# Column means of an 8192 x 8192 matrix: a quarter of the last adds on GpSimd, and the rows loaded in other blocks

## The chip, the core and the metric

The kernel runs on one core of a Trainium2 chip. Its time is device time in microseconds (us), from runs on the chip; lower is better. The engines named here are VectorE (DVE in the profile), GpSimd (POOL), TensorE (PE, with its weight loads as PEld), ScalarE (ACT) and SyncE (SP), which only issues transfers here. SBUF is the on-chip memory, of 128 partitions; PSUM takes TensorE's results. Sixteen DMA engines move data between HBM and SBUF.

## The reference

```python
def reference(x):                 # x: (8192, 8192) float32, standard normal
    return np.mean(x, axis=0)     # 8192 column means
```

All of the 268 MB of `x` has to be read once; the output has 32 KB.

## The kernel before, in words

A *slab* is 128 rows, one in each partition, and so 4 MB in SBUF. There are 64 slabs (`n_slabs`). The first 62 are loaded as 31 *pairs* (`n_pairs`), each of 8 MB: 128 partitions times two rows side by side, 16384 columns, into one of three buffers `pair0` to `pair2` (L48) in turn. Then come slab 62 (`slab`) and slab 63 (`last`), both into the buffer after pair 30's.

**Which rows a pair holds** is free, since all rows are summed. `source` (L78) says it. Rows 0 to 8063 are nine blocks of 7 x 128 rows (`RUN`, L20): partition p has seven rows that lie one after the other in HBM, 224 KB. Pairs 0 to 26 are the first six rows of each partition, two at a time, so a partition's part is one run of 64 KB. The seventh rows of the nine blocks (`single`, L75) make pairs 27 to 30, two blocks for a pair, and slab 62; their runs are 32 KB or less. Slab 63 is the last 128 rows.

**Transfers.** `cuts` (L85) says in how many transfers a pair comes. Pair 0 comes in two, issued by ScalarE (L102 and L139). Pairs 1 to 24 come whole. Pairs 25 to 30 (`BY_ROW`, L19) come by row, 4 MB each, and the last of them in four pieces of half a row. Slab 62 comes in two halves (L161), slab 63 in eight pieces (`PIECES`, L17): 2048, 2048, 2048, 1408, 192, 288, 96 and 64 columns. Apart from pair 0's, all are issued on SP's queue by `load` (L137, L139), in this order. The first transfer of a pair waits until its buffer is free: until the pair three before has been added to the next one (`freed` in the loop, `freed_by` on the semaphore `dve` behind it). What stands behind a waiting transfer on SP waits too.

**VectorE adds.** The running sum moves along: for pair k, an add puts the sum so far (first 8192 columns of the previous buffer) onto the first row of pair k, and a second add puts the second row of pair k onto that. In SBUF, pair k's first 8192 columns are then the sum. Pairs 1 to 24 (`LOOPED`, L21) are in a loop on VectorE (L179 to L189); the rest is the list `adds` (L116 to L134), issued at L192 to L198, each add waiting for the one before it by `dve`. All adds have line L173. At last slab 62 is added to `total` in four parts of 2048 columns, each noted in `done`.

**TensorE ends it.** Matrix products with a column of ones add up over the partitions into PSUM. The columns are four wide parts (2048, 2048, 2048, 1408) and four narrow ones. `open_wide(n)` (L234) waits for `done[n]` and puts `total`'s part into PSUM; `close` (L226) waits for the part's piece of slab 63 and adds it. The order is: some products on zeros (L241, which wait for the second add before `done[0]`), open 0, open 1, close 0, open 2, close 1, open 3 and the narrow ones, close 2, close 3, close narrow (L244 to L256). ScalarE and VectorE multiply by 1/8192 (L266, L269) and four transfers store the result.

GpSimd does nothing in this kernel but four memsets of one column at the start.

Of the kernel before, what the change touches and what calls it, by code (L numbers as in the profile page):

```python
# [7 lines left out]
F32 = mybir.dt.float32  # L8
ADD = mybir.AluOpType.add
MULT = mybir.AluOpType.mult  # L10
P = 128
# [4 lines left out]
NARROW = (192, 288, 96, 64)  # L16
PIECES = WIDE + NARROW  # L17
FIRST = 2048
BY_ROW = 6  # L19
RUN = 7  # L20
LOOPED = 24  # L21


@with_exitstack
def kernel(
# [5 lines left out]
    nc = tc.nc  # L31
    R, C = x.shape
    n_slabs = R // P
    n_pairs = n_slabs // 2 - 1
    N0 = sum(WIDE)
    H = C // 2
    assert n_slabs % 2 == 0 and N0 + sum(NARROW) == sum(PIECES) == C
    assert LOOPED % 3 == 0 and LOOPED < n_pairs - 1
    inv_r = 1.0 / float(R)

    const_pool = ctx.enter_context(tc.tile_pool(name="const", bufs=1))
    psum_pool = ctx.enter_context(
        tc.tile_pool(name="acc", bufs=1, space=bass.MemoryType.PSUM)
    )
    res_pool = ctx.enter_context(tc.tile_pool(name="res", bufs=1))

    ones = const_pool.tile([P, 32], F32, name="ones")
    bufs = [nc.alloc_sbuf_tensor(f"pair{b}", [P, 2 * C], F32, align_bytes=512).ap() for b in range(3)]  # L48
    banks = [psum_pool.tile([P, 512], F32, name=f"bank{b}", tag=f"bank{b}") for b in range(8)]
    rw = nc.alloc_sbuf_tensor("rw", [P, 3 * 512], F32).ap()  # L50
    r3 = nc.alloc_sbuf_tensor("r3", [P, WIDE[3] // GROUPS], F32).ap()
    row = nc.alloc_sbuf_tensor("row", [P, C - N0], F32).ap()[0:1, :]
    idle = res_pool.tile([P, 512], F32, name="idle")

    wide, lo = [], 0
    for n, w in enumerate(WIDE):
# [9 lines left out]

    n_blocks = (R - P) // (P * RUN)
    n_whole = n_blocks * (RUN // 2)  # L70
    assert R == (n_blocks * RUN + 1) * P and 2 * n_whole + n_blocks == 2 * n_pairs + 1
    assert LOOPED < n_whole
    blocks = x[0 : R - P, :].rearrange("(b p j) c -> b p (j c)", p=P, j=RUN)

    def single(n, lo, hi):  # L75
        return blocks[n, :, (RUN - 1) * C + lo : (RUN - 1) * C + hi]

    def source(k, lo, hi):  # L78
        if k < n_whole:
            b, t = divmod(k, RUN // 2)  # L80
            return blocks[b, :, 2 * t * C + lo : 2 * t * C + hi]
        j = lo // C
        return single(2 * (k - n_whole) + j, lo - j * C, hi - j * C)

    def cuts(k):  # L85
        if k == 0:
            return [(0, FIRST), (FIRST, 2 * C)]
        if k < n_pairs - BY_ROW:
            return [(0, 2 * C)]
        step = H if k == n_pairs - 1 else C  # L90
        return [(lo, lo + step) for lo in range(0, 2 * C, step)]

    def untracked(ap, size):

# [2 lines left out]
    sem = nc.alloc_semaphore  # L97
    landed = [sem(f"landed{b}") for b in range(3)]
    first = sem("first")


    early = nc.scalar.dma_start(out=untracked(bufs[0][:, 0:FIRST], 2 * C * P), in_=source(0, 0, FIRST))  # L102
    early.then_inc(first, 16)
    tc.no_tile_sem_insts.add(early.ins.name)
# [4 lines left out]
    with tc.tile_critical(sync_engine=mybir.EngineType.Pool) as section:  # L109
        tc.declare_no_dep(section, early.ins, reason="awaited by first")  # L110
        freed, half = sem("freed"), sem("half")
        dve, act, pe = sem("dve"), sem("act"), sem("pe")
        came = {}


        adds, freed_by = [], {}  # L116
        for k in range(LOOPED + 1, n_pairs):
            pair, before = bufs[k % 3], bufs[(k - 1) % 3]
            pieces = cuts(k)
            for n, (lo, hi) in enumerate(pieces):  # L120
                if lo < C:
                    adds.append(((k, n), pair[:, lo:hi], before[:, lo:hi]))
                else:
                    adds.append(((k, n), pair[:, lo - C : hi - C], pair[:, lo:hi]))
                if hi == C:
                    freed_by[k - 1] = len(adds)
        total = bufs[(n_pairs - 1) % 3]
        slab = bufs[n_pairs % 3][:, 0:C]
        last = bufs[n_pairs % 3][:, C : 2 * C]
        parts = [(lo, lo + 2048) for lo in range(0, C, 2048)]  # L130
        done = []
        for lo, hi in parts:
            adds.append((("slab", lo // H), total[:, lo:hi], slab[:, lo:hi]))
            done.append(len(adds))  # L134


        def load(key, dst, src, after=None):  # L137

            ld = (nc.scalar if key[0] == 0 else nc.sync).dma_start(out=dst, in_=src)  # L139
            if after is not None:  # L140
                ld.wait_op(after[0], after[1], "sem-ge")
            if key not in came:
                came[key] = sem(f"came_{'_'.join(map(str, key))}")
            ld.then_inc(came[key], 16)

        for k in range(n_pairs):
            for n, (lo, hi) in enumerate(cuts(k)):
                after = None
                if k >= 3 and n == 0:
                    f = k - 3  # L150
                    after = (freed, f + 1) if f < LOOPED else (dve, freed_by[f])
                if k == 1:
                    after = (first, 16)
                key = (k, n)
                if k <= LOOPED:
                    came[key] = first if (k, n) == (0, 0) else landed[k % 3]
                if key == (0, 0):
                    continue
                load(key, bufs[k % 3][:, lo:hi], source(k, lo, hi), after)
        r = (n_slabs - 2) * P  # L160
        for n in range(2):  # L161
            after = (dve, freed_by[n_pairs - 3]) if n == 0 else None
            load(("slab", n), slab[:, n * H : n * H + H], single(n_blocks - 1, n * H, n * H + H), after)
        at, lo = {}, 0
        for n, w in enumerate(PIECES):
            load(("last", n), last[:, lo : lo + w], x[r + P : R, lo : lo + w])
# [5 lines left out]
        def vadd(a, b):  # L172
            return nc.vector.tensor_tensor(out=a, in0=a, in1=b, op=ADD)  # L173
# [5 lines left out]
        with nc.vector.register("left") as left:  # L179
            nc.vector.reg_mov(left, LOOPED // 3)  # L180
            with nc.vector.While(lambda: nc.vector.snap(left) > 0):
# [9 lines left out]
        awaited = None  # L191
        for n, (key, a, b) in enumerate(adds):  # L192
            if key != awaited:
                nc.vector.wait_ge(came[key], 16)
                awaited = key
            add = vadd(a, b).then_inc(dve, 1)
# [2 lines left out]
        n_dve = len(adds)  # L199


        n_pe = 0

        def mm(dst, src, **flags):
# [2 lines left out]
        def fold_wide(n, src, **flags):  # L207
            lo, w, bank = wide[n]
            q = w // GROUPS
            for g in range(GROUPS):  # L210
                a = lo + g * q
                m = mm(bank[32 * g : 32 * g + 32, 0:q], src[:, a : a + q], **flags)
            return m
# [12 lines left out]
        def close(fold, n, lo):  # L226
            nonlocal n_pe
            landed_at(lo)
            fold(n, last, start=False, stop=n != narrow[2]).then_inc(pe, 1)
            n_pe += 1  # L230
            return n_pe

        ready = {}
        def open_wide(n):  # L234
            nc.tensor.wait_ge(dve, done[n])
            fold_wide(n, total, start=True, stop=False)


        nc.tensor.wait_ge(dve, done[0] - 2)
        for _ in range(4):  # L240
            nc.tensor.matmul(  # L241
                out=banks[7][:, 0:512], lhsT=idle[:, 0:P], rhs=idle, start=True, stop=True, skip_group_check=True
            )
        open_wide(0)  # L244
        open_wide(1)
        ready["wide", 0] = close(fold_wide, 0, wide[0][0])
        open_wide(2)
        ready["wide", 1] = close(fold_wide, 1, wide[1][0])
        nc.tensor.wait_ge(dve, done[3])
        fold_wide(3, total, start=True, stop=False)  # L250
        for part in (*narrow[:2], ending):
            fold_narrow(part, total, start=True, stop=False)
# [24 lines left out]
        for n, (engine, part) in enumerate(  # L277
            ((nc.scalar, narrow[0]), (nc.vector, narrow[1]), (nc.scalar, ending))
        ):
            lo, w, g, bank, _ = part  # L280
            awaited = ready["narrow", 3 if part is ending else n]
# [68 lines left out]
```

## Time and profile before

| what | us |
|---|---|
| median of 3 runs (lowest, highest) | 627.12 (627.09, 627.58) |
| the profiled execution: time | 627.51 |
| its span, first to last instruction | 625.7 |
| VectorE busy, 67 adds (L173) among it | 541.3, 539.7 |
| VectorE waiting for transfers | 73.7, in 22 waits |
| TensorE busy | 13.6 |
| 4 MB transfers (10), issue to landing, median | 27.6 |

The page has a row for each group of instructions: line, engine, operation, output and input, their shapes, how often; behind the bar the busy time of the group and the mean time of one in ns; behind the second bar the idle time of the engine ahead of them and what ended it. The map of the span has 40 slices, with the busy share in tenths. A timeline's rows begin with start and duration in us, and merge instructions that follow on one another ("x9"). A row of the table of stretches has the stretch, its length, busy time and count for PE, PEld, DVE, ACT and POOL, the granted TensorE clock, the share of the DMA engines and GB/s. The chain of waits goes back from the last instruction to what released each one.

### The profile page before, as it was taken

Reading aid. Unit: us, or ns where it says so; the run is one execution under the profiler, and the core shown is the slowest. Engines: PE = TensorE matmul, PEld = TensorE weight load, DVE = VectorE, ACT = ScalarE, POOL = GpSimd, SP = SyncE. Lnnn points to the kernel's source line nnn. Section 1 sums busy time; section 2 is a strip of 40 time slices with the busy share of each in tenths; the row PEclk is TensorE's granted clock in tenths of the full one; section 3 lists DMA queues with packets and bytes.
Section 4 is the critical chain, followed back from the end, with each engine's and each line's share of the span. In section 5 each row is a group of like instructions: output and inputs, shape, how many; then the busy total and the mean of one; then the engine's idle time right before and its main releaser. Section 6 shows DMA issues by size and latency. Waiting matters only on the chain.

```text
span 625.7 us, 475 instructions
## 1 busy us (share of the span) xinstructions
PE 13.6 (2%) x86; PEld 4.6 (1%) x86; DVE 541.3 (87%) x71; ACT 3.7 (1%) x6; POOL 0.2 (0%) x4
## 2 busy tenths in 40 slices
PE   0000000000000000000000000000000000000025
PEld 0000000000000000000000000000000000000011
DVE  0049999989888899888898888988889899999996
ACT  0000000000000000000000000000000000000001
POOL 0000000000000000000000000000000000000000
PEclk9999999999999999999999999999999999999999
DMA  9999999999999999999999999999999999999997
GB/s 377 436 461 402 469 402 469 402 469 402 469 402 469 402 432 440 402 469 402 469 402 469 402 469 402 469 402 469 402 465 406 432 425 419 434 436 436 434 422 320
DMA packets 7231, 268.48 MB, mean 429 GB/s; under 512 B 1069, under 2 KB 1329, under 8 KB 1470
## 3 DMA queue, kind: packets, MB, share of 16 engines
q1 hardware_dynamic: 6940, 260.08, 96.2%
q10 hardware_dynamic: 290, 8.39, 3.2%
q14 instruction: 1, 0.01, 0.0%
HBM read 268.44 MB, written 0.03 MB: 429 GB/s over the span
## 4 chain that ended last, share of the span: by engine, by line
DMA 59%; DVE 39%; issue 0%; SPq 0%; DVEq 0%; PE 0%; ACTq 0%
DMA pair<-in_x_dram 59%; DVE pair L173 39%; SPq L139 0%; PE bank L205 0%; DVE r L269 0%; DVEq L109 0%; ACTq L102 0%; DVEq L186 0%; DVEq L184 0%; DVEq L173 0%; ACTq L345 0%
## 5 line engine op out<-in xcount | busy, mean ns | idle before, releaser
L173 DVE TENSOR_TENSOR pair<-pair 128x8192 f32<-128x8192 f32 (+2 forms) x67 | 539.7, 8056 | 78.0 <-DMA pair<-in_x_dram 73.7
L241 PE MATMUL bank<-idle 128*128 128x512 f32 x8 | 5.3, 817 | 605.6 <-DVE pair L173 605.6
L205 PE MATMUL bank<-pair,ones 128*32 128x512 f32 (+5 forms) x78 | 8.4, 523 | 3.8 <-DVE pair L173 3.6
L241 PEld LDWEIGHTS bank<-idle 128*128 128x128 f32 x8 | 2.1, 276 | 607.9 <-DVE pair L173 605.6
L266 ACT ACTIVATE rw<-bank 128x512 f32<-128x512 f32 x3 | 1.8, 597 | 617.3 <-PE bank L205 617.3
L269 DVE TENSOR_SCALAR r<-bank 128x352 f32<-128x352 f32 x1 | 0.5, 525 | 3.2 <-PE bank L205 3.2
L205 PEld LDWEIGHTS bank<-pair,ones 128*32 128x32 f32 x78 | 2.5, 108 | 10.2 <-DVE pair L173 7.1
L266 ACT ACT_TABLE_LOAD x1 | 1.3, 1283 | 1.8 <-issue 1.8
L175 DVE MEMSET ones<- 128x32 f32 x1 | 0.1, 85 | 1.0 <-PEq L334 1.0
L266 ACT ACTIVATE row<-bank 1x192 f32<-1x192 f32 (+1 forms) x2 | 0.6, 308 | 0.7 <-PE bank L205 0.7
L176 DVE MEMSET idle<- 128x512 f32 x1 | 0.5, 485 | 0.1
L269 DVE TENSOR_SCALAR row<-bank 1x288 f32<-1x288 f32 x1 | 0.4, 448 | 0.0
L334 POOL MEMSET const-bfloat16-1.0<- 128x1 bf16 x1 | 0.1, 101 | 0.0
L334 POOL MEMSET const-uint8-127<- 128x1 uint8 x1 | 0.1, 101 | 0.0
L334 POOL MEMSET const-float32-0.0<- 128x1 f32 x1 | 0.1, 98 | 0.2 <-issue 0.2
L334 POOL MEMSET const-float32-1.0<- 128x1 f32 x1 | 0.1, 98 | 0.0
## 6 DMA issues: line engine op xcount, KB each, us to landing
pair<-in_x_dram SPq DMA_DIRECT2D x10, 4096.0 KB, 27.6
pair<-in_x_dram SPq DMA_DIRECT2D x6, 2048.0 KB, 28.4
pair<-in_x_dram ACTq DMA_DIRECT2D x1, 7168.0 KB, 37.9
pair<-in_x_dram SPq DMA_DIRECT2D x3, 1024.0 KB, 33.4
pair<-in_x_dram ACTq DMA_DIRECT2D x1, 1024.0 KB, 4.7
pair<-in_x_dram SPq DMA_DIRECT2D x1, 704.0 KB, 36.6
pair<-in_x_dram SPq DMA_DIRECT2D x24, 29.8
pair<-in_x_dram SPq DMA_DIRECT2D x1, 144.0 KB, 30.2
```

The lines of the kernel that those rows point to most:

```text
L173: return nc.vector.tensor_tensor(out=a, in0=a, in1=b, op=ADD)
L175: nc.vector.memset(ones, 1.0)
L176: nc.vector.memset(idle, 0.0)
L205: return nc.tensor.matmul(out=dst, lhsT=ones, rhs=src, skip_group_check=True, **flags)
L241: nc.tensor.matmul(out=banks[7][:, 0:512], lhsT=idle[:, 0:P], rhs=idle, start=True, stop=True, skip_group_check=True)
L266: op = engine.mul(out=dst, in_=src, mul=inv_r).then_inc(act, 1)
L269: op = engine.tensor_scalar(out=dst, in0=src, scalar1=inv_r, scalar2=None, op0=MULT).then_inc(dve, 1)
L334: nc = _bacc.Bacc("TRN2", target_bir_lowering=False, num_devices=1)
```

## The change

- `RUN` is 6: ten blocks of 6 x 128 rows (7680 rows) make pairs 0 to 29, all in runs of 64 KB. The step from one partition's rows to the next one's is 192 KB. Pair 30 is the next 256 rows, two in each partition (`two`), slab 62 the next 128 rows as they lie, slab 63 the last 128.
- Pairs 1 to 29 come whole. Pair 30 comes by row, in two transfers; slab 62 comes in one.
- The loop on VectorE goes to pair 27 (`LOOPED`). Pair 28 is added as before, in adds of 8192 columns.
- For pairs 29 and 30, VectorE adds columns 0 to 4095 and 6144 to 8191, and GpSimd columns 4096 to 6143 (`SHARE`), with a semaphore `gp` of its own. For slab 62, VectorE has three parts of 2048 and GpSimd that of `SHARE`, which is `open_wide(2)`'s.
- GpSimd waits first for VectorE's adds of pair 28 (`whole`), then for each landing, and each add for its own one before.
- SP's load of slab 62 waits for GpSimd's first add as well as for VectorE's.
- `idle` (the zeros of L241) lies in another pool; nothing else is done to it.

```diff
-BY_ROW = 6
-RUN = 7
-LOOPED = 24
+RUN = 6
+LOOPED = 27
+SHARE = (4096, 6144)
...
+    per_block = RUN // 2
+    n_blocks = (n_pairs - 1) // per_block
+    R0 = n_blocks * RUN * P
+    blocks = x[0:R0, :].rearrange("(b p j) c -> b p (j c)", p=P, j=RUN)
+    two = x[R0 : R0 + 2 * P, :].rearrange("(p j) c -> p (j c)", j=2)
 
     def source(k, lo, hi):
-        if k < n_whole:
-            b, t = divmod(k, RUN // 2)
-            return blocks[b, :, 2 * t * C + lo : 2 * t * C + hi]
-        j = lo // C
-        return single(2 * (k - n_whole) + j, lo - j * C, hi - j * C)
+        if k == n_pairs - 1:
+            return two[:, lo:hi]
+        b, t = divmod(k, per_block)
+        return blocks[b, :, 2 * t * C + lo : 2 * t * C + hi]
 
     def cuts(k):
         if k == 0:
             return [(0, FIRST), (FIRST, 2 * C)]
-        if k < n_pairs - BY_ROW:
-            return [(0, 2 * C)]
-        step = H if k == n_pairs - 1 else C
-        return [(lo, lo + step) for lo in range(0, 2 * C, step)]
+        return [(0, C), (C, 2 * C)] if k == n_pairs - 1 else [(0, 2 * C)]
...
+        adds, shared, freed_by = [], [], {}
+        outer = ((0, SHARE[0]), (SHARE[1], C))
         for k in range(LOOPED + 1, n_pairs):
-            pair, before = bufs[k % 3], bufs[(k - 1) % 3]
-            pieces = cuts(k)
-            for n, (lo, hi) in enumerate(pieces):
-                if lo < C:
-                    adds.append(((k, n), pair[:, lo:hi], before[:, lo:hi]))
+            now, before = bufs[k % 3], bufs[(k - 1) % 3]
+            final = len(cuts(k)) - 1
+            for piece, src, lo in ((0, before, 0), (final, now, C)):
+                if k < n_pairs - 2:
+                    adds.append(((k, piece), now[:, 0:C], src[:, lo : lo + C]))
                 else:
-                    adds.append(((k, n), pair[:, lo - C : hi - C], pair[:, lo:hi]))
-                if hi == C:
+                    for a, b in outer:
+                        adds.append(((k, piece), now[:, a:b], src[:, lo + a : lo + b]))
+                    a, b = SHARE
+                    shared.append(((k, piece), now[:, a:b], src[:, lo + a : lo + b]))
+                if not lo:
                     freed_by[k - 1] = len(adds)
+            if k == n_pairs - 3:
+                whole = len(adds)
...
-        for lo, hi in parts:
-            adds.append((("slab", lo // H), total[:, lo:hi], slab[:, lo:hi]))
-            done.append(len(adds))
+        for lo in range(0, C, 2048):
+            cols = slice(lo, lo + 2048)
+            if (lo, lo + 2048) == SHARE:
+                shared.append((("slab", 0), total[:, cols], slab[:, cols]))
+                done.append((gp, len(shared)))
+            else:
+                adds.append((("slab", 0), total[:, cols], slab[:, cols]))
+                done.append((dve, len(adds)))
...
-        for n in range(2):
-            after = (dve, freed_by[n_pairs - 3]) if n == 0 else None
-            load(("slab", n), slab[:, n * H : n * H + H], single(n_blocks - 1, n * H, n * H + H), after)
+        nc.sync.wait_ge(gp, 1)
+        load(("slab", 0), slab, x[r : r + P, :], (dve, freed_by[n_pairs - 3]))
...
+        nc.gpsimd.wait_ge(dve, whole)
+        awaited = None
+        for n, (key, a, b) in enumerate(shared):
+            if key != awaited:
+                nc.gpsimd.wait_ge(came[key], 16)
+                awaited = key
+            add = nc.gpsimd.tensor_tensor(out=a, in0=a, in1=b, op=ADD).then_inc(gp, 1)
+            if n:
+                add.wait_op(gp, n, "sem-ge")
...
         def open_wide(n):
-            nc.tensor.wait_ge(dve, done[n])
+            nc.tensor.wait_ge(*done[n])
```

More of the change, by code (lines that the diff above doesn't have):

```diff
@@ L35 @@
     N0 = sum(WIDE)
-    H = C // 2
     assert n_slabs % 2 == 0 and N0 + sum(NARROW) == sum(PIECES) == C
-    assert LOOPED % 3 == 0 and LOOPED < n_pairs - 1
+    assert LOOPED % 3 == 0 and LOOPED < n_pairs - 2
     inv_r = 1.0 / float(R)
@@ L44 @@
     )
-    res_pool = ctx.enter_context(tc.tile_pool(name="res", bufs=1))
     ones = const_pool.tile([P, 32], F32, name="ones")
+    idle = const_pool.tile([P, 512], F32, name="idle")
     bufs = [nc.alloc_sbuf_tensor(f"pair{b}", [P, 2 * C], F32, align_bytes=512).ap() for b in range(3)]
@@ L52 @@
     row = nc.alloc_sbuf_tensor("row", [P, C - N0], F32).ap()[0:1, :]
-    idle = res_pool.tile([P, 512], F32, name="idle")
     wide, lo = [], 0
@@ L65 @@
     ending = (narrow[2][0], sum(NARROW[2:]), narrow[2][2], narrow[2][3], 0)
[L69 to L76, printed above, removed]
-    def source(k, lo, hi):
-        if k < n_whole:
-            b, t = divmod(k, RUN // 2)
-            return blocks[b, :, 2 * t * C + lo : 2 * t * C + hi]
-        j = lo // C
-        return single(2 * (k - n_whole) + j, lo - j * C, hi - j * C)
+    per_block = RUN // 2
+    n_blocks = (n_pairs - 1) // per_block
+    R0 = n_blocks * RUN * P
+    assert n_blocks * per_block == n_pairs - 1 and R == R0 + 4 * P
+    blocks = x[0:R0, :].rearrange("(b p j) c -> b p (j c)", p=P, j=RUN)
+    two = x[R0 : R0 + 2 * P, :].rearrange("(p j) c -> p (j c)", j=2)
+    def source(k, lo, hi):
+        if k == n_pairs - 1:
+            return two[:, lo:hi]
+        b, t = divmod(k, per_block)
+        return blocks[b, :, 2 * t * C + lo : 2 * t * C + hi]
     def cuts(k):
@@ L111 @@
         freed, half = sem("freed"), sem("half")
-        dve, act, pe = sem("dve"), sem("act"), sem("pe")
+        dve, act, pe, gp = sem("dve"), sem("act"), sem("pe"), sem("gp")
         came = {}
-        adds, freed_by = [], {}
+        adds, shared, freed_by = [], [], {}
+        outer = ((0, SHARE[0]), (SHARE[1], C))
         for k in range(LOOPED + 1, n_pairs):
-            pair, before = bufs[k % 3], bufs[(k - 1) % 3]
-            pieces = cuts(k)
-            for n, (lo, hi) in enumerate(pieces):
-                if lo < C:
-                    adds.append(((k, n), pair[:, lo:hi], before[:, lo:hi]))
-                else:
-                    adds.append(((k, n), pair[:, lo - C : hi - C], pair[:, lo:hi]))
-                if hi == C:
+            now, before = bufs[k % 3], bufs[(k - 1) % 3]
[3 more added lines that the diff above has]
+                    adds.append(((k, piece), now[:, 0:C], src[:, lo : lo + C]))
+                else:
+                    for a, b in outer:
[3 more added lines that the diff above has]
+                if not lo:
                     freed_by[k - 1] = len(adds)
+            if k == n_pairs - 3:
+                whole = len(adds)
         total = bufs[(n_pairs - 1) % 3]
@@ L129 @@
         last = bufs[n_pairs % 3][:, C : 2 * C]
-        parts = [(lo, lo + 2048) for lo in range(0, C, 2048)]
         done = []
-        for lo, hi in parts:
-            adds.append((("slab", lo // H), total[:, lo:hi], slab[:, lo:hi]))
-            done.append(len(adds))
+        for lo in range(0, C, 2048):
[6 more added lines that the diff above has]
+                done.append((dve, len(adds)))
         def load(key, dst, src, after=None):
@@ L234, in open_wide @@
         def open_wide(n):
-            nc.tensor.wait_ge(dve, done[n])
+            nc.tensor.wait_ge(*done[n])
             fold_wide(n, total, start=True, stop=False)
-        nc.tensor.wait_ge(dve, done[0] - 2)
+        nc.tensor.wait_ge(dve, done[0][1] - 2)
         for _ in range(4):
@@ L248 @@
         ready["wide", 1] = close(fold_wide, 1, wide[1][0])
-        nc.tensor.wait_ge(dve, done[3])
+        nc.tensor.wait_ge(*done[3])
         fold_wide(3, total, start=True, stop=False)
```

## The prediction, on record before the result

> **What bounds the kernel now.** I read the page's busy shares, the chain of waits, the groups by form, the timeline of the last 40 us, and table-of-stretches answers for the transfer rate.
>
> ```profile
> PE 13.6 (2%) x86; PEld 4.6 (1%) x86; DVE 541.3 (87%) x71; ACT 3.7 (1%) x6; POOL 0.2 (0%) x4
> DMA  9999999999999999999999999999999999999997
> ...
> DMA 59%; DVE 39%; issue 0%; SPq 0%; DVEq 0%; PE 0%; ACTq 0%
> ```
> The DMA engines are full in every slice but the last: 268.4 MB move from 1.30 us (first transfer of the chain) to 621.63 us, 433 GB/s. The chain names DVE for 39% only because a free buffer and a landing alternate in it; no slice shows the transfers starved. VectorE has 541 us of work, so it keeps up, with little to spare.
>
> From the groups by form:
> ```profile
> L173 DVE TENSOR_TENSOR pair<-pair 128x8192 f32<-128x8192 f32 x59 | 512.9, 8692 | 77.7 <-DMA pair<-in_x_dram 73.7
> L173 DVE TENSOR_TENSOR pair<-pair 128x4096 f32<-128x4096 f32 x4 | 17.7, 4424 | 0.1
> L173 DVE TENSOR_TENSOR pair<-pair 128x2048 f32<-128x2048 f32 x4 | 9.2, 2292 | 0.1
> ...
> L334 POOL MEMSET const-float32-1.0<- 128x1 f32 x1 | 0.1, 98 | 0.0
> L175 DVE MEMSET ones<- 128x32 f32 x1 | 0.1, 85 | 1.0 <-PEq L334 1.0
> ```
> An add costs 1.042 ns a column ((8692 - 2292)/6144) plus 0.16 us. A pair takes 2 x 8.7 = 17.4 us of VectorE. The chain shows one wait on DMA in two pairs ending every 38.7 us (147.38 + 29.72 = 177.10, then 215.81, 254.71 and so on), so a pair lands every 19.34 us: 433.7 GB/s. POOL's only rows are four one-column memsets.
>
> The last 40 us, from the timelines of DVE and of all engines:
> ```profile
> 556.56 26.15 DVE L173 TENSOR_TENSOR pair<-pair 128x8192 f32<-128x8192 f32 x3
> 583.48 35.84 DVE L173 TENSOR_TENSOR pair<-pair 128x8192 f32<-128x8192 f32 x9 [0.77 <-DMA pair<-in_x_dram]
> ```
> ```profile
> 612.39 1.06 PE L205 MATMUL bank<-pair,ones 128*32 128x512 f32 x8 [1.53 <-DVE pair L173]
> ...
> 614.71 1.92 PE L205 MATMUL bank<-pair,ones 128*32 128x512 f32 x16 [1.26 <-DVE pair L173]
> ...
> 617.04 1.92 PE L205 MATMUL bank<-pair,ones 128*32 128x512 f32 x16 [0.40 <-DVE pair L173]
> ...
> 619.37 2.13 PE L205 MATMUL bank<-pair,ones 128*32 128x352 f32 x22 [0.40 <-DVE pair L173]
> ...
> 621.67 1.32 PE L205 MATMUL bank<-pair,ones 128*32 128x352 f32 x16 [0.18 <-DMA pair<-in_x_dram]
> ```
> Two ends meet here. Pair 29's second row landed just before 583.48; the last piece landed at 621.63: four 4 MB rows in 38.2 us, 9.55 us each. So pair 30 was in by about 593.0 and 602.5, slab 62 by 612.1. VectorE has no gap from 583.48 to 619.32 (8.69 + 4 x 4.42 + 4 x 2.29, with 0.03 between), and PE is through with its part at 621.50, 0.13 us ahead of the landing. **Transfers set the end, but VectorE and PE stand 0.1 us behind them.** Before 583.48 VectorE had already done pair 29's first row, 8.7 us of work, because that row was a transfer of its own.
>
> **What the change does to this, part by part.** Times are those of the profiled execution: span 625.7, time 627.51 (1.8 around the span); the shown runs have the median 627.12, so its sum may stand 0.4 high.
>
> *Transfers.* Pairs 25 to 29 go from 32 KB runs to 64 KB, pair 30 and slab 62 from 16 to 32 KB; eight issues of SP fall away (0.33 to 0.43 us each, all under a full queue: nothing; if the queue were dry, 3 us). Rates by stretch, GB/s last in each row (64 KB runs, 32 KB, and the 16 KB stage):
>
> ```profile
> 39.20:483.20 444.00, 0.00 (x0) 0.00 (x0) 406.87 (x47) 0.00 (x0) 0.00 (x0) 1.00 1.00 432
> ...
> 523.30:542.60 19.30, 0.00 (x0) 0.00 (x0) 19.23 (x3) 0.00 (x0) 0.00 (x0) 1.00 1.01 435
> ...
> 600.00:610.00 10.00, 4.40 (x7) 2.06 (x8) 9.93 (x3) 0.00 (x0) 0.00 (x0) 1.00 0.99 423
> ```
> The other stretches between 483.2 and 600 have 430 to 435. So 32 to 64 KB gives nothing that can be read, and 16 to 32 KB about 2.4% of 10 us, **-0.2 us**, with bounds 0 and -0.5. The blocks of six rows instead of seven change the step between partitions in HBM, from 224 to 192 KB, for the whole stream. The trace has steps of 224 KB (433.7 GB/s) and, in the last slab, of 32 KB (431 in 610 to 616, with small pieces): a difference of 0.6%, so between 0 and +/-3.9 us on 620. I take 0, the row of the same run length.
>
> *Pairs 25 to 28 whole.* VectorE starts a pair when all of it is in, 17.4 of 19.34 us: 1.9 us idle per pair, on no path. Pair 30's load now waits for pair 28's first add, at 564.1 + 8.7 = 572.8, and the queue is full until 583.4: free, unless that add comes 10 us late.
>
> *Pair 29 whole.* Its first add moves from 574.0 to 583.45, so 8.7 us of VectorE's work is put behind that point. That is what GpSimd is to pay for: VectorE has 4 half pairs of 4.42 + 2.29 = 6.71, and 3 x 2.29 for the slab: 33.7 us, 34.1 with gaps, against 35.84 now. GpSimd has five adds of 2048 columns.
>
> *GpSimd's add.* No row shows one. From below 2.29 us, VectorE's row of the same shape. From above 4.42, VectorE's row of 4096 columns: an engine that fetches its two operands one after the other makes as many fetches. I take 4.27 (4096 x 1.042, without the fixed part): POOL's memset of one column takes 98 ns where VectorE's of 32 takes 85, so it is not the quicker engine. [...]
>
> *Beside or in turn.* This decides. VectorE's rate of one column per 1.04 ns with two inputs is about what its memset without inputs has (512 columns in 485 ns): it fetches two operands at once, with no room shown for a third reader. PE's matmuls read SBUF beside the slab's adds, and those stay at 2292 ns; that is another engine's path. Cost from both sides: nothing (fully beside; a gain is excluded, no add of VectorE's becomes quicker) up to all five adds added to VectorE's time. To come out even the change needs three things at once: VectorE not slowed, GpSimd's add under about 6.3 us, its first one done by 600. I take **in turn**, whole adds or single fetches, which sums the same:
>
> 583.45 + 34.1 + 5 x 4.27 = 638.9 for VectorE's last add, against 619.32. No gap opens: pair 30 (602.5) and slab 62 (612.1) are in when their turn comes, and the slab load, which SP issues after GpSimd's first add and VectorE's first two of pair 29 (583.45 + 6.71 + 4.27 to 8.5 = 595 to 599), still goes before the queue is empty at 602.5. Behind that wait stand the last slab's eight loads, at 0.48 each, and the stores.
>
> *PE.* It gets the parts closer together. Parts 0, 1, 3 come from VectorE at 2.3 us intervals; at the second, PE still owes open 1, close 0, open 2, close 1, part 3 with the narrow ones, close 2 and close 3. That is 1.92 + 1.72 + 1.93 + 1.16 = 6.7 us (the rows above, less about 0.2 of start-up each where they follow on without a gap); before, it took 8.3 (614.71 to 622.99) with waits for VectorE in it. Second part in turn: 638.9 - 2.3 = 636.6, so PE ends at 643.3; 622.99 before: **+20.3**. What follows PE (drains and stores, 2.7 us to the span's end) stays. The transfers' -0.2 doesn't count here, since they are no longer last. Sum: 627.5 + 20.3 = **647.8 us**. With GpSimd's add at 2.29: 9.9 less, 637.9. At 4.42 with gaps of 0.1 at each hand-over: about 650.
>
> [...]
>
> **Rivals.**
>
> *A, beside each other (not slower).* GpSimd's rows have no reader beside them, so nothing excludes it. Then VectorE does pair 29 in 583.45 to 596.9, pair 30 to 603.6 and 610.4, waits for slab 62 at 612.1 - 0.2, and its parts come at 614.2, 616.5 and 618.8; GpSimd's at 616.2. PE: 616.5 + 6.7 = 623.2 against 622.99, +0.2. Time 627.7; 627.3 as seen from the median. Range 626.3 to 628.8. It holds up to a GpSimd add of 6.3 us (612.0 to 618.3, when PE comes to open 2); each us above that is a us of time.
>
> *B, VectorE always goes first.* If GpSimd gets its turn only when VectorE is idle, its first add comes after 610.4, is done by 614.7, and the slab load, which waits for it, starts with an empty queue: 2.3 us of latency (the first 1 MB took 4.7 from issue to landing, 2.4 of it at full rate), then 2 x 9.6. Last landing 636.2 to 637, and GpSimd still owes four adds: 643 to 647.
>
> *C, the six-row step.* At the 431 of the other step: +3.9 us where A holds, 631. The contrary, 0.3% more rate, 626.
>
> **Numbers.** In turn 0.47 (own range 637 to 651), A 0.33, B 0.12, C slower 0.04, C faster 0.04. At 435 GB/s, the best stretch of 19.3 us, the transfers would need 617.1 us and 2.3 of latency, 0.9 less than their 620.3 now, so faster by over 0.2% (1.25 us; about what a measurement of this kernel can tell from no change) is nearly shut out: 0.06 with A's lower edge. Same: 0.28, from A. Slower: 0.66. The range takes in A's and the forecast's: 626.3 to 651.
>
> **What would show it.** In turn: VectorE's 4096-column adds after 583 far above 4.42 us, or gaps before them while their data is in; GpSimd's adds filling those; DVE done near 639; PE idle on DVE until then. Beside: 4.42 and 2.29 unchanged, last add near 619, PE closing without a gap. B: SP's slab load issued after 610 and a DMA slice below 9. C: landings in the middle not 38.7 us apart. Wrong is the forecast if VectorE's mean per column stays at 1.04 ns with GpSimd busy.

## The result, and the profile after

| | before | changed |
|---|---|---|
| median (lowest, highest) of 6 runs, us | 627.29 (627.0, 627.7) | 647.18 (646.66, 647.54) |
| the profiled execution: time, span | 627.51, 625.7 | 646.66, 644.9 |

The changed kernel is slower: ratio 1.0316, 95% interval 1.0302 to 1.0329. The forecast was 647.8 us: 0.6 above this median, and 1.1 above the profiled execution, for which its sum was made.

The groups by form of the changed kernel (adds of VectorE are now L175, those of GpSimd L210):

```profile
L175 DVE TENSOR_TENSOR pair<-pair 128x8192 f32<-128x8192 f32 x57 | 495.5, 8692 | 83.7 <-DMA pair<-in_x_dram 79.6
L210 POOL TENSOR_TENSOR pair<-pair 128x2048 f32<-128x2048 f32 x5 | 38.7, 7737 | 582.6 <-DMA pair<-in_x_dram 582.3
L175 DVE TENSOR_TENSOR pair<-pair 128x2048 f32<-128x2048 f32 x7 | 28.6, 4081 | 0.2
L175 DVE TENSOR_TENSOR pair<-pair 128x4096 f32<-128x4096 f32 x4 | 26.0, 6512 | 2.0 <-DMA pair<-in_x_dram 1.9
```
An add of 8192 columns takes 8692 ns as before. Those of 4096 and 2048 columns, which run beside GpSimd's, have means of 6512 and 4081 ns; before they had 4424 and 2292. Hardly any of it shows as idle time: **what VectorE loses is shown in these rows as a longer instruction, not as a later one.** A mean hides how; the single instructions show it. First VectorE's timeline from pair 29's landing on (start, duration; each row from a window of its own, since a timeline merges them):

```profile
582.73 4.43 DVE L175 TENSOR_TENSOR pair<-pair 128x4096 f32<-128x4096 f32 x1 [1.89 <-DMA pair<-in_x_dram]
587.19 6.47 DVE L175 TENSOR_TENSOR pair<-pair 128x2048 f32<-128x2048 f32 x1
593.69 8.60 DVE L175 TENSOR_TENSOR pair<-pair 128x4096 f32<-128x4096 f32 x1
602.32 6.47 DVE L175 TENSOR_TENSOR pair<-pair 128x2048 f32<-128x2048 f32 x1
608.82 8.60 DVE L175 TENSOR_TENSOR pair<-pair 128x4096 f32<-128x4096 f32 x1
617.45 6.47 DVE L175 TENSOR_TENSOR pair<-pair 128x2048 f32<-128x2048 f32 x1
623.95 4.42 DVE L175 TENSOR_TENSOR pair<-pair 128x4096 f32<-128x4096 f32 x1
628.41 2.29 DVE L175 TENSOR_TENSOR pair<-pair 128x2048 f32<-128x2048 f32 x1
...
635.39 2.29 DVE L175 TENSOR_TENSOR pair<-pair 128x2048 f32<-128x2048 f32 x1
```
And GpSimd's timeline over the same time:

```profile
582.77 8.73 POOL L210 TENSOR_TENSOR pair<-pair 128x2048 f32<-128x2048 f32 x1 [582.33 <-DMA pair<-in_x_dram]
591.58 6.42 POOL L210 TENSOR_TENSOR pair<-pair 128x2048 f32<-128x2048 f32 x1
598.08 8.55 POOL L210 TENSOR_TENSOR pair<-pair 128x2048 f32<-128x2048 f32 x1
606.71 6.42 POOL L210 TENSOR_TENSOR pair<-pair 128x2048 f32<-128x2048 f32 x1
613.21 8.55 POOL L210 TENSOR_TENSOR pair<-pair 128x2048 f32<-128x2048 f32 x1
```
Read the two together. VectorE's first add has its own 4.43 us; GpSimd's, issued 0.04 later, lasts until 591.50, 4.3 us after VectorE's ended. VectorE's second add, of 2.29 us, takes 6.47, 4.18 too long: it ends 2.16 after GpSimd's has ended. GpSimd's second, issued at 591.58, ends at 598.00, 4.34 after that. So it goes, one instruction of each in turn, five times: each of the five adds of VectorE that follow a GpSimd add is 4.18 us too long, 20.9 us in sum. When GpSimd has no more adds (from 621.76 on), VectorE's have 4.42 and 2.29 again. The last of them ends at 637.7.

TensorE's timeline, the two rows behind the products on zeros (matrix products whose result nobody uses):

```profile
633.67 1.06 PE L218 MATMUL bank<-pair,ones 128*32 128x512 f32 x8
635.41 6.64 PE L218 MATMUL bank<-pair,ones 128*32 128x512 f32 x70 [0.68 <-DVE pair L175]
```
All 70 remaining products run without a gap: PE waits for VectorE and for no landing. The transfers were over long before, as the table of stretches shows (DMA share and GB/s at the end of the row):

```profile
581.30:621.25 39.95, 0.00 (x0) 0.00 (x0) 38.35 (x6) 0.00 (x0) 38.16 (x5) 1.00 0.98 420
621.25:637.70 16.45, 8.59 (x40) 3.03 (x44) 16.27 (x6) 0.29 (x1) 0.52 (x1) 1.00 0.00 0
```

### The profile page after: what moved, and what is told of

The parts are those of the page before. It is cut to its first block, busy times and chain, and to the rows that moved or that the text cites. A ratio compares the mean times of both kernels' runs of the same rounds, so it can differ in the third digit from the quotient of the medians.

```text
span 644.9 us, 482 instructions
## 1 busy us (share of the span) xinstructions
PE 12.9 (2%) x86; PEld 5.2 (1%) x86; DVE 551.6 (86%) x72; ACT 3.7 (1%) x6; POOL 38.9 (6%) x9
## 4 chain that ended last, share of the span: by engine, by line
DMA 65%; DVE 33%; PE 1%; issue 0%; DVEq 0%; ACTq 0%
DMA pair<-in_x_dram 65%; DVE pair L175 32%; PE bank L218 1%; DVE r L282 0%; DVEq L101 0%; DVEq L188 0%; ACTq L94 0%; DVEq L186 0%; DVEq L175 0%; ACTq L358 0%; DVEq L196 0%
## 5 line engine op out<-in xcount | busy, mean ns | idle before, releaser
L175 DVE TENSOR_TENSOR pair<-pair 128x8192 f32<-128x8192 f32 (+1 forms) x68 | 550.1, 8089 | 86.0 <-DMA pair<-in_x_dram 81.5
L210 POOL TENSOR_TENSOR pair<-pair 128x2048 f32<-128x2048 f32 x5 | 38.7, 7737 | 582.6 <-DMA pair<-in_x_dram 582.3
L218 PE MATMUL bank<-pair,ones 128*32 128x512 f32 (+6 forms) x78 | 7.7, 518 | 0.7 <-DVE pair L175 0.7
```

The costliest lines, as they stand in the source:

```text
L210: add = nc.gpsimd.tensor_tensor(out=a, in0=a, in1=b, op=ADD).then_inc(gp, 1)
L218: return nc.tensor.matmul(out=dst, lhsT=ones, rhs=src, skip_group_check=True, **flags)
```

## The experiments

The experiments test this theory, **turns**: a GpSimd add and a VectorE add, each with two operands in SBUF, exclude one another for a whole instruction, and each GpSimd add holds VectorE back by its own 4.2 us. Rivals: the time is lost by the loads (pairs 29 and 30 whole, other blocks), or GpSimd is in VectorE's way by any access to SBUF, or only by its first use.

**Without GpSimd.** The changed kernel, but VectorE adds the quarter too.

```diff
-                if k < n_pairs - 2:
+                if k < n_pairs:
                     adds.append(((k, piece), now[:, 0:C], src[:, lo : lo + C]))
...
-        nc.sync.wait_ge(gp, 1)
...
-        nc.gpsimd.wait_ge(dve, whole)
-        ...
```

> The changed kernel without GpSimd: VectorE does pairs 29 and 30 in adds of 8192 columns and slab 62 in four parts of 2048; all loads as changed. Turns (a GpSimd add holds VectorE's next add back by its own 4.2 us): VectorE's last add at 582.7 + 4 x 8.72 + 4 x 2.32 = 626.9, PE done 3.7 later as in the kernel before, so 7.6 over the kernel before: 635, that is 12 us faster than with GpSimd's help. Rival (the loss is from pair 29 and 30 landing whole, GpSimd takes nothing away): as slow as the changed kernel or slower, 647 to 657.

Measured 635.31 us, ratio to before 1.0123 (1.0108 to 1.0139). Taking GpSimd's help away makes the changed kernel 11.9 us faster. VectorE's stretch, from pair 29's first add to the last add, is 44.18 us instead of 54.96:

```profile
583.12 44.18 DVE L170 TENSOR_TENSOR pair<-pair 128x8192 f32<-128x8192 f32 x8 [1.89 <-DMA pair<-in_x_dram]
```
What is left over the kernel before, 7.9 us, is the price of the whole loads without help: pair 29's first add comes 9 us later. Some 2 us of it are PE's: its 70 products took 8.73 us instead of 6.64, at a granted clock of 0.50 in 620.5 to 623 (more on this below).

**The quarter on TensorE.** The changed kernel; PE folds columns 4096 to 6143 of the sum up to pair 28, of pairs 29 and 30 and of slab 62 into PSUM as they land.

```diff
-        nc.gpsimd.wait_ge(dve, whole)
-        ...
...
+        nc.tensor.wait_ge(dve, whole)
+        fold_wide(2, src[:, 0:C], start=True, stop=False).then_inc(gp, 1)
+        awaited = None
+        for key, a in quarter:
+            if key != awaited:
+                nc.tensor.wait_ge(came[key], 16)
+                awaited = key
+            fold_wide(2, a, start=False, stop=False)
```

> The changed kernel with the quarter (columns 4096 to 6143) of pairs 29, 30 and slab 62 added up by TensorE in PSUM instead of by GpSimd; loads and VectorE's adds as changed. Turns between VectorE and GpSimd as the cause: TensorE takes no turn, VectorE's adds stay at 4.42 and 2.29 us, its last one ends near 619, and the time is that of the rival case of the prediction, 626.5 to 627.7. Rival (any second reader of these buffers, or the whole loads, cost the time): adds of VectorE longer than 4.42 and 2.29, 635 or more.

Measured 628.25 us, ratio 1.0013 (1.0004 to 1.0022). VectorE's groups by form in this kernel:

```profile
L174 DVE TENSOR_TENSOR pair<-pair 128x4096 f32<-128x4096 f32 x4 | 17.7, 4426 | 2.0 <-DMA pair<-in_x_dram 1.9
L174 DVE TENSOR_TENSOR pair<-pair 128x2048 f32<-128x2048 f32 x7 | 16.0, 2292 | 2.1 <-DMA pair<-in_x_dram 1.9
```
Same loads, same adds of VectorE, another helper: the adds have 4426 and 2292 ns, and 19 of the 20 us are gone. It is not the loads, and not just any second reader. The time is 0.6 above the range that was expected. PE's end shows where it comes from:

```profile
608.07 6.56 PE L254 MATMUL bank<-idle 128*128 128x512 f32 x8 [3.55 <-DVE pair L174]
614.63 1.07 PE L206 MATMUL bank<-pair,ones 128*32 128x512 f32 x8
616.96 6.91 PE L206 MATMUL bank<-pair,ones 128*32 128x512 f32 x70 [1.26 <-DVE pair L174]
```
The products on zeros (first row) ran at a low granted clock, 0.56 in 608 to 614.6, but that cost nothing here: behind the first part PE still waited 1.26 us for VectorE. The second part came at 616.96 (616.5 in rival A of the prediction), since slab 62 was waited for until 612.19, and PE needed 6.91 us from there (6.7 in A).

**GpSimd with the loads of before.** The kernel before, and only the share put in.

```diff
+                    for c, d in ((0, SHARE[0]), (SHARE[1], C)):
+                        if a <= c and d <= b:
+                            adds.append(((k, n), pair[:, c:d], src[:, off + c : off + d]))
+                    c, d = SHARE
+                    if a <= c and d <= b:
+                        shared.append(((k, n), pair[:, c:d], src[:, off + c : off + d]))
```

> The kernel before, with its loads, and only GpSimd's share put in (same columns, pairs 29 and 30 and slab 62). Turns: five adds of GpSimd's take 5 x 4.19 from VectorE and spare it 5 x 2.32, 9.4 net, so its last add ends at 628.7 and PE gets the parts closer together: about 637, 10 over the kernel before. Rival (only the loads matter): 627, or less by the help.

Measured 640.7 us, ratio 1.0213 (1.0198 to 1.0229): the direction is that of the turns, but 3.7 us more than expected. VectorE's last add starts at 626.4 and ends at 628.7, as expected; the miss is PE's. The table of stretches (PEclk is the third number from the right):

```profile
615.30:620.40 5.10, 5.09 (x8) 1.98 (x8) 5.10 (x1) 0.00 (x0) 4.29 (x1) 1.00 1.01 424
620.40:624.10 3.70, 0.00 (x0) 0.00 (x0) 3.63 (x3) 0.00 (x0) 0.00 (x0) 1.00 0.38 128
624.10:626.40 2.30, 1.14 (x8) 0.16 (x8) 2.29 (x1) 0.00 (x0) 0.00 (x0) 0.69 0.00 0
626.40:628.00 1.60, 1.56 (x8) 0.40 (x12) 1.58 (x1) 0.00 (x0) 0.00 (x0) 0.50 0.00 0
```
PE was through with its products on zeros at 620.4, and had nothing to do for 3.7 us because VectorE was late. Then the granted clock fell to 0.50, and the 70 products took 9.28 us, not 6.64. Whether the clock is the reason, the next run tests.

**The same, PE kept busy:** eight products on zeros instead of four.

```diff
-        for _ in range(4):
+        for _ in range(8):
```

> The kernel with the loads of before and GpSimd's share, with eight products on zeros instead of four ahead of the folds. It had measured 640.7 where 637 was expected; its PE had waited 3.7 us between the products on zeros and the first fold, the granted clock stood at 0.50 from then to 631, and the folds took 9.28 us from the second part where the changed kernel's took 6.64. If that is the excess: clock 1.00, folds 6.7, 638.1. Rival (the excess is GpSimd's): 640.7 again.

Measured 637.77 us, ratio 1.0166 (1.0150 to 1.0181). The clock stays at 1.00 from 620 on, and the 70 products take 6.64 us:

```profile
626.64 6.64 PE L231 MATMUL bank<-pair,ones 128*32 128x512 f32 x70 [0.19 <-DVE pair L188]
```
So the miss was the clock, and GpSimd's share alone costs the kernel before 10.6 us. VectorE loses by the turns here too: adds of 4096 and 2048 columns that wait for a whole GpSimd add have 8.61 and 6.48 us in its chain of waits.

**Six-row blocks alone.** The kernel before, with its cuts and VectorE alone, the rows from six-row blocks.

```diff
-RUN = 7
+RUN = 6
...
-            load(("slab", n), ..., single(n_blocks - 1, n * H, n * H + H), after)
+            load(("slab", n), ..., x[r : r + P, n * H : n * H + H], after)
```

> The kernel before, VectorE alone, transfers cut as before (pairs 25 to 29 by row, pair 30 and slab 62 by half rows), but rows taken in six-row blocks, pair 30 from two-row blocks and slab 62 from the rows as they lie. If the 0.8 us by which the transfers end earlier in the changed kernel come from the six-row step, a pair lands every 19.31 us here too (19.34 before) and the last transfers end near 621.3, time 626.5 to 627.2; if they come from the longer runs at the end, the last transfers end near 622.0 as before and the time is 627.3. Rival C of the prediction (the step costs 0.6%): 631.

Measured 627.22 us, ratio 0.9999 (0.9990 to 1.0008). The step between the partitions' rows makes no difference that can be read, and rival C's 3.9 us are out. In the profiled execution the landing that the end waited for stood at 621.19 (before: 621.63); one execution each does not say whether that is the blocks.

**What excludes what.** Trials ahead of the kernel before, in the third buffer: operations of VectorE (first in each bracket) and GpSimd (second) alone and side by side, released by one semaphore. `gadd` is GpSimd's add of 2048 columns, `gset` its memset. `two`, `one` and `none` are a VectorE add, multiply and memset of 6144 columns, with two, one and no operands in SBUF; `bank` is six VectorE adds with the second operand in PSUM.

```diff
+        for v, g in (
+            (None, gadd), (None, gadd), (two, None), (two, gadd),
+            (None, gset), (two, gset),
+            (one, None), (one, gadd),
+            (none, None), (none, gadd),
+            (bank, None), (bank, gadd),
+        ):
```

> The kernel before with trials put in ahead of it, in the third buffer, whose first load waits for their end; so its time is longer by them and says nothing. Each trial is run alone and side by side, released by one semaphore. Turns over a shared read path: GpSimd's add of 2048 columns alone about 4.3 us; beside a VectorE add of 6144 columns (6.56 us, two SBUF inputs) it ends 4.2 to 4.3 us after VectorE's, so shows about 10.8; beside a VectorE multiply with one SBUF input, a VectorE memset, or VectorE adds with the second input in PSUM, it shows about 4.3 as alone, and VectorE's are unchanged; a GpSimd memset (reads nothing) beside VectorE's add changes neither. Rival (GpSimd is slowed by any VectorE work, or every access to SBUF): 10.8 or a stretched duration in all five.

The time of this kernel, 676.09 us, has the trials in it. From its timelines, the GpSimd add alone, then five pairs:

```profile
19.93 4.49 POOL L189 TENSOR_TENSOR pair<-pair 128x2048 f32<-128x2048 f32 x1 [19.50 <-DVE bank L185]
...
35.62 6.56 DVE L195 TENSOR_TENSOR pair<-pair 128x6144 f32<-128x6144 f32 x1
35.67 10.86 POOL L189 TENSOR_TENSOR pair<-pair 128x2048 f32<-128x2048 f32 x1 [6.67 <-DVE pair L195]
...
48.43 6.56 DVE L195 TENSOR_TENSOR pair<-pair 128x6144 f32<-128x6144 f32 x1 [6.25 <-POOL pair L192]
48.45 1.80 POOL L192 MEMSET pair<- 128x2048 f32 x1
...
58.42 3.36 DVE L198 TENSOR_SCALAR pair<-pair 128x6144 f32<-128x6144 f32 x1
58.47 7.66 POOL L189 TENSOR_TENSOR pair<-pair 128x2048 f32<-128x2048 f32 x1 [8.21 <-DVE pair L198]
...
72.73 4.50 POOL L189 TENSOR_TENSOR pair<-pair 128x2048 f32<-128x2048 f32 x1 [6.60 <-DVE pair L201]
74.00 5.18 DVE L201 MEMSET pair<- 128x6144 f32 x1 [1.35 <-issue]
...
82.92 3.68 DVE L206 TENSOR_TENSOR pair<-pair,bank 128x512 f32<-128x512 f32 x6
82.97 4.52 POOL L189 TENSOR_TENSOR pair<-pair 128x2048 f32<-128x2048 f32 x1 [5.74 <-DVE pair L206]
```
The GpSimd add needs 4.49 us alone. Beside a VectorE add with two SBUF operands it ends 4.35 us after VectorE's end (46.53 against 42.18): it ran afterwards. A GpSimd memset, which reads nothing, changes nothing (1.80 and 6.56 us, as alone). A VectorE memset beside GpSimd's add costs nothing either (5.18 us as alone; it came 1.3 us late, so 3.2 us of it lie beside the add), nor do VectorE's adds with the second operand in PSUM (3.68 us for six, as alone). Against the expectation, VectorE's multiply with one SBUF operand also excludes GpSimd's add (7.66 = 3.36 + 4.3). It runs at 0.55 ns a column (3.36 us for 6144), about twice the add's rate. So it is not GpSimd as such, nor SBUF as such, that is in the way: in these trials GpSimd's add was held back beside VectorE's two-operand add and multiply (10.86 and 7.66 us), and not beside VectorE's memset and VectorE's adds with a PSUM operand (4.50 and 4.52). Why these and not the others, and whether a read path is shared, the trials do not show.

**Two adds instead of five.** GpSimd's share for pair 29 alone; VectorE waits for these two adds before it goes on to pair 30.

```diff
-                if k < n_pairs - 2:
+                if k != n_pairs - 2:
...
+            if n + 1 == freed_by[n_pairs - 3] + 2:
+                nc.vector.wait_ge(gp, 2)
```

> The changed kernel with GpSimd's quarter for pair 29 alone (two adds instead of five); VectorE does pair 30 and slab 62 whole. Turns, one for one: VectorE's stretch from pair 29's landing to its last add is 44.18 us without GpSimd and 54.96 with five turns; here 4.44 + 6.48 + 8.61 + 2.31 + 4 x 8.72 wait: two rows of pair 30 make two adds of 8.71, slab four of 2.33, so 4.44 + 6.48 + 8.61 + 2.31 + 17.42 + 9.3 = 48.6. Its last add near 631.5, PE slow at the granted clock of 0.5 as in the run without GpSimd: about 639.5. Rival (a fixed cost of the first use of GpSimd, not one for each add): 52 us or more.

Measured 640.27 us in one run, where about 639.5 was expected. VectorE's stretch is 48.64 us, as expected:

```profile
583.00 48.64 DVE L171 TENSOR_TENSOR pair<-pair 128x4096 f32<-128x4096 f32 x10 [1.90 <-DMA pair<-in_x_dram]
```
It is 44.18 without GpSimd, 48.64 with two adds, 54.96 with five. That is 2.2 us an add (4.46 / 2 and 10.78 / 5): 4.2 of turn, less 2.1 that VectorE is spared per add, plus about 0.16 for the cut of its add into two. A fixed cost of first use does not show.

**A version that beats both?** Three kernels took the whole loads, gave the quarter to PE as above, and let PE fold all of slab 62 as well, so that nothing but landings is left at the end.

```diff
+        for src, start in ((total, True), (slab, False)):
+            if src is slab:
+                nc.tensor.wait_ge(came["slab", 0], 16)
+            for n in (0, 1, 2, 3):
+                if n != 2 or src is slab:
+                    fold_wide(n, src, start=start, stop=False)
```

> The quarter on TensorE as before, and TensorE also folds all of slab 62, so VectorE's last add is pair 30's, near 610.3, and PE waits for the last landing alone. If the whole loads in longer runs are worth anything once no adder stands behind them, the end is the last landing (621.2 to 622.0) plus 1.3 for PE and 2.7 behind it: 626.3 to 627.2, at or below the kernel before. Rival (PE has become the bound): PE closes without waiting for the last landing, 628 or more.

Measured 628.14 us, ratio 1.0016 (1.0007 to 1.0025). PE waited 1.4 us for a landing behind close 1, the clock fell to 0.50 (621.4 to 623.4), and the last 24 products took 3.95 us. So products on zeros were put into that wait:

```diff
             ready["wide", n] = close(fold_wide, n, wide[n][0])
+            for _ in range((0, 3, 0, 0)[n]):
+                nc.tensor.matmul(out=banks[7][:, 0:512], lhsT=idle[:, 0:P], rhs=idle, ...)
```

> The kernel in which TensorE takes the quarter and slab 62, with three more products on zeros behind close 1, where PE had waited 1.4 us for a landing and its granted clock had then gone to 0.50 for the last closes (3.95 us for 24 products). If the lower clock is what it lost: clock 1.00 to the end, the last closes 1.3 us behind the last landing, 626.5 to 627.2, no slower than the kernel before. Rival (PE bound by its own work, or by later landings): 628 as without them.

Measured 628.69 us, ratio 1.0025 (1.0015 to 1.0035). Clock 1.00, but no gain: three products take 2.84 us where the wait was 1.4, and so close 2 starts at 621.86 instead of 620.43. These 1.4 us are most of what the clock had cost (24 products in 3.95 us, now 2.13). With one (`(0, 1, 0, 0)`):

> As the last, with one product on zeros behind close 1 instead of three. Three had kept the clock at 1.00 but took 2.8 us where the wait is 1.4, and so put close 2 at 621.86 instead of 620.4. One takes about 0.9: if the clock holds, close 2 starts at the landing, the last closes end 1.3 us behind the last landing, and the time is 626.6 to 627.5, the kernel before's. Rival (the short gap left is enough for the clock to fall): 628.

Measured 628.11 us, ratio 1.0015 (1.0006 to 1.0024), above the expected range once more. PE now does what was meant, at clock 1.00, and its chain ends in a landing alone:

```profile
591.57 30.71 DMA pair<-in_x_dram
622.28 0.04 issue
622.33 0.84 PE bank L198 x8
```
The landing that the end waits for is at 622.28, against 621.63 before. The same stretch of both kernels, first before, then this one (the DMA share is the last number but one):

```profile
621.75:622.00 0.25, 0.25 (x6) 0.08 (x9) 0.00 (x0) 0.25 (x1) 0.00 (x0) 1.00 0.96 248
621.75:622.00 0.25, 0.00 (x0) 0.00 (x0) 0.00 (x0) 0.23 (x1) 0.00 (x0) 1.00 0.05 15
```
From 621.5 to 622.5 the share is 0.05 to 0.13 here, which is what one or two engines of 16 would make, while before it falls from 0.96 to 0.13 only at 622.0. So most of the transfers are done earlier and a few packets come late. Which packets, and why, stays open; none of these kernels beats the one before, which stays the fastest, with the six-row variant level with it.

## Why the prediction was right, point by point

- **Pair 29's first add, 583.45:** measured 582.73. Single executions with these loads have 582.73 to 583.33, so up to 0.6 of the 0.7 can be scatter; all of them are earlier than the prediction had it.
- **In turn, not beside:** shown by the two timelines, by the pairs, and by its absence when PE is the helper. It was chosen with a chance of 0.47 against 0.33 for rival A, so by little, and the reason taken from the trace is weaker than it looked. It was that VectorE's add, at 1.04 ns a column, goes at about its memset's rate, so that it fetches two operands at once and leaves no room for a third reader. The trials have 0.84 ns a column for a long memset (5.18 us for 6144), and the multiply, with one operand, excludes GpSimd too, which this reason does not foresee. Nor could any row of the kernel before show the two engines side by side, so that they take turns was the author's estimate. The choice was right, but this argument does not carry it, and in part it was luck. Whole adds or single fetches was left open; the runs show whole adds.
- **GpSimd's add, 4.27 us between 2.29 and 4.42:** it takes VectorE 4.18 a turn. Alone it has 4.49, just above the upper bound. The argument by fetches (as many as a VectorE add of 4096 columns) hit the size; that fetches are the reason is not shown. The turn is 0.3 less because the instructions overlap a little at each change: GpSimd's ends 4.34 after VectorE's, VectorE's 2.16 after GpSimd's (2.29 by itself).
- **VectorE's last add at 638.9:** 637.7. The sum is 0.7 high from the landing and 0.45 from the turns (5 x 0.09).
- **PE 6.7 us from the second part:** 6.64. End of PE 642.05 against 643.3, and the span 644.9 against 646.0 by the sum. The 6.7 takes full clock for granted (see the last point).
- **Slab load issued at 595 to 599, before the queue is dry:** it went out at 593.7, and the last of the nine loads by 599.1; the DMA share was 0.97 in 595 to 600, 1.04 in 600 to 610 and 0.95 in 610 to 618, so the queue did not run dry. GpSimd started on slab 62 at 613.21, straight after its add before; the landing was not waited for. So B (VectorE always first) did not happen: VectorE's and GpSimd's instructions alternate, in five turns of five.
- **Transfers, -0.2 us, and six-row blocks, 0:** no gain can be read in any time. The -0.2 took the stretch 600 to 610, with 423 GB/s, for the 16 KB stage. By the prediction's own landings pair 30 and slab 62, in such runs, moved from 583.5 to 612.1, and the stretch 581.3 to 600 has 434 GB/s. The term did not enter the sum. The blocks alone give 0.9999 (0.9990 to 1.0008). The bulk of the transfers did end some 0.7 us earlier in the changed kernel, hidden here behind VectorE; the last kernel above, which could have used it, had a late landing instead.
- **What the whole loads cost without help** was put at 8.7 us of VectorE's work behind the landing; the kernel without GpSimd shows 8.0 us in VectorE's last add (627.3 against 619.3) and 7.9 us of time. Leaving the help out would have been the better kernel of the two.
- **A step the prediction did not have:** PE's clock. It did no harm in the changed kernel: its products on zeros ended at 633.7, the first part, ready at 633.0, followed without a gap, and the granted clock was 1.00 from 628 to 642. As far as the prediction goes that was luck: in the two experiments with gaps of 3.7 and 5.4 us ahead of the first part the clock was at 0.50 behind it (626.4 to 630 and 620.5 to 623), and the 70 products took 2.6 and 2.1 us more.

## What to carry to other kernels

Before giving an engine a helper, ask whether the two can run at the same time with their operands where they are. Here two adds with operands in SBUF did not: each add of 2048 columns moved from VectorE to GpSimd cost VectorE 4.2 us and saved it 2.1. Look for the loss in the durations of single instructions, since neither idle time (0.2 us ahead of the seven adds of 2048 columns) nor the waits showed it here, and compare an instruction with its own shape elsewhere. And try by a run whether another idle engine can do the same work: TensorE took this quarter without lengthening any of VectorE's adds, and the kernel was then 0.1% slower than before instead of 3.2%.

## What the runs showed of the hardware that was not expected

- The exclusion was by whole instructions and strictly in turn: in five turns of five of the changed kernel, VectorE's next add, started 0.03 us after its last one ended, did not get ahead of a GpSimd add that was already waiting.
- VectorE's multiply with one operand in SBUF (0.55 ns a column) excluded GpSimd's add as the two-operand add did (7.66 us); beside VectorE adds with one operand in PSUM, GpSimd's add has 4.52 us against 4.49 alone.
- TensorE's granted clock fell to 0.50 after gaps of 3.7 us (GpSimd with the loads of before) and 5.4 us (without GpSimd); in the kernel whose slab 62 TensorE folds, after waits of 0.4 and 1.4 us close together (0.50 from 621.4 to 623.4). A gap of 1.5 us in the kernel before left it at 1.00 (612.3 to 617). How long a gap it takes, these runs do not settle.
